# Entry of the down-projection: queue order of weights, operands, convolutions and loads

## The chip, the cores and the metric

The kernel runs on one core of one Trainium2 chip. The metric is the device time of one execution in microseconds; the time before is the median of three runs. The profile shows one execution: TensorE (PE) does the matmuls, ScalarE (ACT), VectorE (DVE) and GpSimd (POOL) the elementwise work, and SyncE (SP) issues most of the DMAs. Each engine works through its own queue in order, and so does SP: what waits at the head of a queue holds what is behind it.

## The reference

One decoder layer on a sequence of 1024 positions of width 1024, in float32: an RMSNorm, two attention mixers with gates and a residual addition, and then the part that matters here:

```
xn = rmsnorm(x, norm_ffn_w)
u = xn @ w_up                                  # 1024 -> 2 * 2816
c = conv_b + sum_j upad[:, j:j + S] * conv_w[j]  # causal, width 3, per channel
gate, val = split(c, 2)
x = x + (silu(gate) * val) @ w_down            # 2816 -> 1024
out = rmsnorm(x, norm_final_w)
```

## The kernel before

Activations lie transposed, channels on the 128 partitions and positions along the free dimension (T = 1024, in halves of H2 = 512). Every float32 matmul is done as three fp32r matmuls: each operand is split into a head (a cast, by ACT) and the rest (source less head, by DVE), and head x head, head x rest and rest x head are summed. For weights the two parts are `wh` and `wl` (`load_w`, lines 139 and 141), for operands of the down-projection the two halves of `h` (`split`, lines 820 and 821). Two by two blocks are multiplied in Strassen's manner with seven products, P1 to P7, whose operands are sums of blocks.

**Up-projection** (`hidden`). 22 iterations, j = 0 to 21, each a pair of weight columns and seven products of twelve matmuls (line 901). `recombine` (lines 460 to 467) sums the products into two tiles `us`. `glu` then does, for each of the pair, `conv`: a product with the norm's scale by POOL (line 1047), the first tap with the bias on ACT (line 1056), two further taps on DVE (lines 1058 and 1059); then silu on ACT (line 1039), a product on DVE (line 1040) and a store of the hidden row tile to `hd` in DRAM (line 1041). Three `glu` calls at the end are put off into the list `self.defer`: the second half of j = 20 and both halves of j = 21. The argument `after` makes such a call's POOL product wait for an instruction, the `wl` of some weight.

**Down-projection** (`down`). Its loop runs over steps i = 0, 1, 2, ...: for each of the products P1, P2, P5, P6, P3, P7, P4 two cuts of the 11 row tiles of a block (6 and 5), and for each cut four column blocks m. A step is 18 or 15 matmuls at line 1112: P1 is steps 0 to 7 (written as `y`), P2 is steps 8 to 15 (written as `d`). A step needs its weights and six or five operands. After a chain's second cut its bank is added to `x3`, the residual, by DVE (line 1118), one step later.

A step of the loop issues, in this order of the program: `next_w` (it keeps two steps of weights split: ACT's cast and DVE's rest of the following step, and the raw loads, at line 129, of two more); its matmuls; at steps 2, 10, 18 and 26 a load of 1 MB of the residual from `x2d` (line 1149); the loads of raw hidden tiles from the table `loads` (`fetch_h`, line 999: tiles `ha`, `hb`, `hc` for the blocks B11, B12 and B21/B22); as many operand preparations as the table `count` or a rule says (`prep`, calling `operand`: for P5 the subtraction at line 1020, for P6 the one at line 1022, and then the split); a deferred `glu` at the steps in `DEFER`; a late store of `hd` at the steps in `STORE`; evictions.

The six operands of P1's first cut are loaded during j = 20 (line 971) into tiles of the up-projection. The other five, B11 6 to 10, are loaded at steps 0 and 1. `open_down` makes the pools of the raw tiles (`hrp`, 11 buffers of each kind) in the space of the up-projection's operands, and one of the pools of split operands (`hp`, HP buffers); the other (`hpb`, HPB buffers) lies in the space of the up-projection's split weights and `us` tiles.

What sets the order. The program is a list; a planner with a cost model for each instruction lays out each engine's queue before the run, taking what it holds to be ready, the earliest in the list first. `tc.high_priority(n)` moves a block's instructions n places forward in that order. `with tc.issue_after(ins):` forces the block's instructions that are on the engine of `ins` to stand behind it in that engine's queue. Nothing is reordered during the run. `self.front`, a pair of instructions, does the same for the first ACT and the first DVE operation of the next convolution.

Of the kernel before, what the change touches and what calls it, by code (L numbers as in the profile page):

```python
# [22 lines left out]
H2 = 512  # L23
DFF = 2816
NF = DFF // P
EPS = 1e-6
RAW = 3
HP, HPB, HR = 6, 14, 11
STORE = (1, 6)
DEFER = (2, 5)  # L30
HK = NF // 2
# [13 lines left out]
class Trunk:  # L45
# [858 lines left out]
    def hidden(self, pair):  # L904
        nc, tc = self.nc, self.tc
        with ExitStack() as ctx:
# [11 lines left out]
            for j in range(NF):  # L918
                w, ps = ready.pop(j) if j else (w0, {})
                if j == 0:  # L920
# [4 lines left out]
                    for k in range(4):  # L925
                        hi, lo = self.split(*(xc2.tile([P, T], F32R, name=f"T42_{k}{p}") for p in "hl"), self.t42[k])
                        self.B["T4", k], self.B["T2", k] = ((hi[:, c], lo[:, c]) for c in (slice(0, H2), slice(H2, T)))
                    self.tctx.close()
                    tp = e(tc.tile_pool(name="tp", bufs=2, side="right", reuse_waits="tile"))
# [21 lines left out]
                if j == NF - 1:  # L951
                    self.defer.pop(0)(lo)
                    self.xctx2.close()
                    self.uw = None
                    self.open_down()
                    self.deep = True
                    with tc.high_priority(100):
                        self.ahead(2)
                self.recombine(ps, us, tp, 2)
                if j < NF - 1:  # L960
# [19 lines left out]
                if j > NF - 3:  # L980
                    self.front = None

                for w in range(2):
                    f = lambda after=None, j=j, w=w, us=us: self.glu(j, w, us[w], tp, after)
                    if j + w < NF - 1:
                        f()
                    else:
                        self.defer.append(f)

    def open_down(self):  # L990
        tc = self.tc
        self.dctx = ExitStack()
        self.hrp = self.dctx.enter_context(tc.tile_pool(name="hrp", bufs=HR, reuse_waits="tile"))
        self.hp = self.dctx.enter_context(tc.tile_pool(name="hp", bufs=HP, reuse_waits="tile"))
        self.nh = 0

# [46 lines left out]

    def conv(self, m, us, tp, after=None):
        nc = self.nc
        nc.gpsimd.memset(us[:, 0:2], 0.0)
        i = (nc.vector if m % NF == 0 else nc.gpsimd).tensor_tensor(us[:, 2:], us[:, 2:], self.rstd, ALU.mult)  # L1047
        if after is not None:
            self.tc.add_manual_dep(i.ins, after.ins.name, mybir.DependencyInfo(mybir.DependencyClass.Sync, mybir.DependencyReason.DATA), reason="later")
        c = self.tl(self.cpl, [P, T], "c")  # L1050
        cw = [self.vecs[:, C_CW + 3 * m + k:C_CW + 3 * m + k + 1] for k in range(3)]

        cast, low = [self.tc.issue_after(i) for i in self.front] if self.front else [nullcontext()] * 2
        self.front = None
        with cast:
            nc.scalar.activation(c, us[:, 2:], AF.Identity, bias=self.vecs[:, C_CB + m:C_CB + m + 1], scale=cw[2])  # L1056
        with low:
            nc.vector.scalar_tensor_tensor(c, us[:, 1:T + 1], cw[1], c, ALU.mult, ALU.add)  # L1058
        nc.vector.scalar_tensor_tensor(c, us[:, 0:T], cw[0], c, ALU.mult, ALU.add)  # L1059
        return c  # L1060

    def down(self):

        nc, tc = self.nc, self.tc
        with ExitStack() as ctx:
# [3 lines left out]
            self.hpb = e(tc.tile_pool(name="hpb", bufs=HPB, side="right", reuse_waits="tile"))  # L1069
            self.B, self.R = {("P1", k): self.hs[k] for k in range(6)}, {}  # L1070
            tt = nc.vector.tensor_tensor
# [7 lines left out]
            def fetch(name, *ks):  # L1079
                for k in ks:  # L1080
                    self.fetch_h(name, k)
# [34 lines left out]
            def evict(ps, m, hf, done):  # L1116
                x = col(m, hf)
                tt(x, x, ps, ALU.subtract if m > 3 else ALU.add)
                if done:
# [4 lines left out]

            loads = {0: [("B11", 6, 7, 8)], 1: [("B11", 9, 10)], 2: [("B21", 0, 1)], 3: [("B21", 2, 3)], 4: [("B21", 4, 5)], 5: [("B21", 6, 7)],
                     6: [("B21", 8, 9)], 7: [("B21", 10), ("B11", 0)]}
            for k in range(11):
                loads.setdefault(8 + k // 2, []).append(("B12", k))
                loads.setdefault(14 + k // 2, []).append(("B22", k))
            for k in range(1, 6):  # L1130
                loads[7 + k].insert(0, ("B11", k))
            count = {0: 3, 1: 2, 3: 1, 6: 3, 7: 2}
            chains, owed, tail, i = [{}, {}], [], [], 0
            for stage in STAGES:
                which, start, o, hf, done = plan[stage]
                for c in range(2):
                    for m in range(4):
                        if stage == "P4" and c == 1 and m > 1:
                            break
                        with tc.high_priority(150 if i < 4 else 0):  # L1140
                            w = self.next_w()
# [5 lines left out]
                        if i % 8 == 2 and i < 32:  # L1147
                            r, h = ((0, 0), (4, 1), (0, 1), (4, 0))[i // 8]
                            nc.sync.dma_start(x3[:, r:r + 4, h * H2:(h + 1) * H2], self.x2d[r:r + 4, :, h * H2:(h + 1) * H2].rearrange("m p t -> p m t"))
                        if i > 1:  # L1150
                            for l in loads.get(i, ()):
                                fetch(*l)
                        for k, _ in again:
                            fetch("B21", k)
                        again.clear()
                        if i < 2:
                            fetch(*loads[i][0])
                        prep(count.get(i, 0) if i < 8 else 2 if i % 4 < 2 or i < 16 else 1)
                        if i in DEFER:
                            self.defer.pop(0)(lo)  # L1160
                        if i in STORE:
# [136 lines left out]
```

## Time and profile before

| | us |
|---|---|
| median of three runs | 1335.62 (1335.47 to 1339.52) |
| profiled execution | 1335.52 |
| span of its profile | 1333.7 |
| PE busy | 1312.1 |
| DVE busy | 1056.9 |
| ACT busy | 621.2 |
| POOL busy | 479.5 |

The span runs from the first to the last instruction of the profile. Busy times of engines overlap each other. Matmuls are pipelined: an interval from start to start is the time that one costs, and the duration of a record, about 0.39 us, is longer than that. In a row of the timeline the first number is the start, the second the duration; a bracket at its end gives how long the engine had been idle just before and what it had waited for.

### The profile page before, as it was taken

The page shows a single profiled execution, that of the slowest core. Times are in us where ns is not written, and L with a number is a line of the kernel's source. Part 1 is how long each engine was busy: PE and PEld are TensorE (multiplying, and loading weights), DVE is VectorE, ACT ScalarE, POOL GpSimd, SP SyncE. Part 2 cuts the span into 40 slices and gives each one's busy share as a digit, 9 for nine tenths or more (in the row PEclk, how much of TensorE's full clock was granted, in tenths as well). Part 3 has the DMA queues.
Part 4 walks back from the last instruction along what each step waited for, and adds up shares of the span by engine and source line. Part 5 has one row for each costly group of instructions (what it writes and reads, how often), then busy time and mean ns, then how long its engine had stood idle before and what let it go on. Part 6 is the DMA issues. An engine that isn't in the chain of part 4 may idle for free.

```text
span 1333.7 us, 17123 instructions
## 1 busy us (share of the span) xinstructions
PE 1312.1 (98%) x6210; PEld 1090.0 (82%) x6210; DVE 1056.9 (79%) x1456; ACT 621.2 (47%) x967; POOL 479.5 (36%) x364
## 2 busy tenths in 40 slices
PE   9999999999999999999999999999999997999997
PEld 7888888888888878888888888888888885788886
DVE  8846775389898976455669999999999996998545
ACT  9432232276667774334444343334343434554543
POOL 0446652000101015641446666756666621000002
PEclk9999999999999999999999999999999999999998
DMA  7334342966553245234424336644635228864334
GB/s 259 129 147 153 141 158 111 274 173 190 143 149 136 76 143 223 101 122 142 151 90 180 121 138 166 145 186 123 220 101 150 71 91 274 303 204 155 96 97 146
DMA packets 71588, 205.96 MB, mean 154 GB/s; under 512 B 8016, under 2 KB 15824, under 8 KB 71376
## 3 DMA queue, kind: packets, MB, share of 16 engines
q1 hardware_dynamic: 57472, 176.03, 38.9%
q0 software_dynamic: 2304, 11.54, 4.5%
q10 hardware_dynamic: 11728, 17.31, 3.6%
q8 instruction: 49, 0.80, 0.2%
q14 instruction: 35, 0.29, 0.1%
HBM read 156.08 MB, written 71.83 MB: 171 GB/s over the span
## 4 chain that ended last, share of the span: by engine, by line
PE 82%; DVE 7%; issue 4%; DMA 2%; POOL 2%; ACT 2%; SPq 0%; POOLq 0%; DVEq 0%; ACTq 0%
PE t L901 32%; PE y L1112 7%; PE d L1112 7%; PE g L160 4%; PE g L161 4%; PE g L162 4%; PE sc L161 3%; PE sc L162 3%; PE sc L160 3%; PE sc L633 3%; DVE wl L120 1%; DVE c L1058 1%; PE t L649 1%; DVE c L1059 1%; PE t L752 1%
## 5 line engine op out<-in xcount | busy, mean ns | idle before, releaser
L141 DVE TENSOR_TENSOR wl<-raw,wh 128x1024 fp32r<-128x1024 f32 (+2 forms) x85 | 97.3, 1145 | 52.7 <-ACT wh L139 43.0
L139 ACT CAST wh<-raw 128x1024 fp32r<-128x1024 f32 (+2 forms) x85 | 74.1, 873 | 130.2 <-PE y L1112 53.5
L1047 POOL TENSOR_TENSOR us<-us,rstd 128x1024 f32<-128x1024 f32 x42 | 93.4, 2257 | 58.4 <-DVE us L466 31.5
L1056 ACT ACTIVATE c<-us,vecs 128x1024 f32<-128x1024 f32 x44 | 54.8, 1248 | 121.9 <-POOL us L1047 113.0
L120 DVE TENSOR_TENSOR sl<-sf,sh 128x1024 fp32r<-128x1024 f32 x62 | 95.9, 1548 | 14.7 <-ACT sh L118 14.7
L118 ACT CAST sh<-sf 128x1024 fp32r<-128x1024 f32 x62 | 64.7, 1046 | 85.7 <-PE t L901 44.0
L177 POOL TENSOR_TENSOR rs<-ms,mhalf 128x8 f32<-128x8 f32 (+2 forms) x9 | 13.3, 1474 | 235.8 <-DVE ms L175 229.7
L104 POOL TENSOR_TENSOR sf<-rv 128x512 f32<-128x512 f32 x30 | 54.9, 1830 | 117.6 <-DMA rv<-in_w_up 57.4
L1112 PE MATMUL y<-h,wh 128*128 128x512 f32 (+1 forms) x324 | 96.1, 380 | 0.0
L1112 PE MATMUL d<-h,wh 128*128 128x512 f32 x264 | 81.3, 389 | 0.2 <-ACT wh L139 0.2
L1059 DVE SCALAR_TENSOR_TENSOR c<-us,vecs,c 128x1024 f32<-128x1024 f32 x44 | 74.4, 1724 | 0.0
L160 PE MATMUL g<-xh,wh 128*128 128x512 f32 x176 | 70.9, 403 | 1.5 <-ACT g L562 1.5
L161 PE MATMUL g<-xl,wh 128*128 128x512 f32 x176 | 70.3, 400 | 0.0
L162 PE MATMUL g<-xh,wl 128*128 128x512 f32 x176 | 70.3, 399 | 0.0
L1112 PEld LDWEIGHTS y<-h,wh 128*128 128x128 f32 x324 | 60.1, 190 | 11.3
L106 POOL TENSOR_TENSOR sf<-raw,rv 128x512 f32<-128x512 f32 x30 | 54.9, 1830 | 35.6 <-DVE sl L120 35.6
L1058 DVE SCALAR_TENSOR_TENSOR c<-us,vecs,c 128x1024 f32<-128x1024 f32 x44 | 64.3, 1490 | 4.1 <-ACT c L1056 3.9
L1112 PE MATMUL y<-h,wl 128*128 128x512 f32 (+1 forms) x162 | 61.9, 382 | 3.3 <-DVE wl L141 3.2
L120 DVE TENSOR_TENSOR wl<-raw,wh 128x1024 fp32r<-128x1024 f32 (+1 forms) x32 | 62.8, 1962 | 0.1
L637 DVE CUSTOM_DVE_ANT_0 L<-sc,bias 128x128 f32<-128x128 f32 (+7 forms) x64 | 47.7, 750 | 17.0 <-PE sc L633 13.7
L616 POOL MEMSET aT<- 128x128 f32 x32 | 6.2, 206 | 151.7 <-PE t L662 97.9
L638 ACT ACTIVATE L<-L,sm 128x128 f32<-128x128 f32 (+7 forms) x64 | 49.6, 778 | 19.9 <-DVE sm L637 17.3
(394 smaller groups left out, 4159.3 us busy)
## 6 DMA issues: line engine op xcount, KB each, us to landing
u<-qd SPq DMA_DIRECT2D x72, 256.0 KB, 6.2
raw<-in_w_up SPq DMA_DIRECT2D x23, 512.0 KB, 4.9
raw<-in_w_in SPq DMA_DIRECT2D x22, 512.0 KB, 3.8
hd<-c SPq DMA_DIRECT2D x22, 512.0 KB, 2.6
sdP<-in_w_down POOLq DMA_DIRECT2D x16, 704.0 KB, 9.2
rv<-in_w_up SPq DMA_DIRECT2D x21, 512.0 KB, 4.6
hc<-hd SPq DMA_DIRECT2D x33, 256.0 KB, 5.3
gr<-gd SPq DMA_DIRECT2D x16, 512.0 KB, 3.4
```

The source lines that it names most:

```text
L118: cast = nc.scalar.copy(hi, src)
L120: low = nc.vector.tensor_tensor(lo, src, hi.bitcast(F32), ALU.subtract)
L139: self.hi = nc.scalar.copy(wh, raw)
L141: self.lo = (eng or nc.vector).tensor_tensor(wl, raw, wh.bitcast(F32), ALU.subtract)
L160: nc.tensor.matmul(ps, wh[:, kc + o, :], ah, start=first and n == 0, stop=False)
L161: nc.tensor.matmul(ps, wh[:, kc + o, :], al, start=False, stop=False)
L162: nc.tensor.matmul(ps, wl[:, kc + o, :], ah, start=False, stop=last and n == len(kcs) - 1)
L901: nc.tensor.matmul(ps, (ah, ah, al)[p][:, k, :], (bh, bl, bh)[p], start=first and n == p == 0, stop=last and p == 2 and n == len(ks) - 1, ...
L1047: i = (nc.vector if m % NF == 0 else nc.gpsimd).tensor_tensor(us[:, 2:], us[:, 2:], self.rstd, ALU.mult)
L1058: nc.vector.scalar_tensor_tensor(c, us[:, 1:T + 1], cw[1], c, ALU.mult, ALU.add)
L1059: nc.vector.scalar_tensor_tensor(c, us[:, 0:T], cw[0], c, ALU.mult, ALU.add)
L1112: nc.tensor.matmul(ps, v[:, k - k0, :], x, start=start and k == i == 0, stop=k == HK - 1 and i == 2, skip_group_check=True)
```

## The change

It changes the order around the entry of the down-projection, j = 21 and steps 0 to 7, and ties operand preparations to weights in all steps.

- At j = 21 the five loads B11 6 to 10 are issued ahead of the next weights, and the first deferred `glu` comes after these weights, with `self.front` set: its ACT and DVE taps stand behind the weights' cast and rest.
- The scale product of the last two convolutions is a function of its own, `scaled`, called at steps 2 and 4; the rest of each convolution follows one step later (3 and 5), with `self.front` set to that step's weights.
- The table `loads` starts with B21 0 to 5 at steps 0 and 1. The weights of step 1's `next_w`, where they are on SP, stand behind the last of the loads of step 0, and the residual's loads stand behind the last operand load.
- In every step the preparations stand behind the latest `wh` and `wl` on ACT and DVE.
- One operand preparation moves from step 6 to step 4. The pools of split operands have 7 and 13 buffers where they had 6 and 14.

```diff
-HP, HPB, HR = 6, 14, 11
+HP, HPB, HR = 7, 13, 11
 STORE = (1, 6)
-DEFER = (2, 5)
+DEFER = (2, 4)
...
                 if j == NF - 1:
-                    self.defer.pop(0)(lo)
                     self.xctx2.close()
                     self.uw = None
                     self.open_down()
                     self.deep = True
                     with tc.high_priority(100):
+                        for k in range(6, HK):
+                            self.fetch_h("B11", k)
                         self.ahead(2)
+                    self.front = self.hi.ins, self.lo.ins
+                    self.defer.pop(0)(lo)
                 self.recombine(ps, us, tp, 2)
...
-    def conv(self, m, us, tp, after=None):
+    def scaled(self, m, us, after=None):
         nc = self.nc
         nc.gpsimd.memset(us[:, 0:2], 0.0)
         i = (nc.vector if m % NF == 0 else nc.gpsimd).tensor_tensor(us[:, 2:], us[:, 2:], self.rstd, ALU.mult)
         if after is not None:
             self.tc.add_manual_dep(i.ins, after.ins.name, mybir.DependencyInfo(mybir.DependencyClass.Sync, mybir.DependencyReason.DATA), reason="later")
+
+    def conv(self, m, us, tp, after=None):
+        nc = self.nc
+        if m % NF < NF - 1:
+            self.scaled(m, us, after)
         c = self.tl(self.cpl, [P, T], "c")
...
-            loads = {0: [("B11", 6, 7, 8)], 1: [("B11", 9, 10)], 2: [("B21", 0, 1)], 3: [("B21", 2, 3)], 4: [("B21", 4, 5)], 5: [("B21", 6, 7)],
-                     6: [("B21", 8, 9)], 7: [("B21", 10), ("B11", 0)]}
+            loads = {0: [("B21", 0, 1, 2)], 1: [("B21", 3, 4, 5)], 4: [("B21", 6, 7)], 6: [("B21", 8, 9)], 7: [("B21", 10), ("B11", 0)]}
...
-            count = {0: 3, 1: 2, 3: 1, 6: 3, 7: 2}
+            count = {0: 3, 1: 2, 3: 1, 4: 1, 6: 2, 7: 2}
...
-                        with tc.high_priority(150 if i < 4 else 0):
+                        with tc.high_priority(150 if i < 4 else 0), tc.issue_after(self.load.ins) if i == 1 else nullcontext():
                             w = self.next_w()
                         lo = self.lo
...
                         if i % 8 == 2 and i < 32:
                             r, h = ((0, 0), (4, 1), (0, 1), (4, 0))[i // 8]
-                            nc.sync.dma_start(x3[:, r:r + 4, h * H2:(h + 1) * H2], self.x2d[r:r + 4, :, h * H2:(h + 1) * H2].rearrange("m p t -> p m t"))
-                        if i > 1:
-                            for l in loads.get(i, ()):
-                                fetch(*l)
+                            with tc.issue_after(self.load.ins):
+                                nc.sync.dma_start(x3[:, r:r + 4, h * H2:(h + 1) * H2], self.x2d[r:r + 4, :, h * H2:(h + 1) * H2].rearrange("m p t -> p m t"))
+                        for l in loads.get(i, ()):
+                            fetch(*l)
                         for k, _ in again:
                             fetch("B21", k)
                         again.clear()
-                        if i < 2:
-                            fetch(*loads[i][0])
-                        prep(count.get(i, 0) if i < 8 else 2 if i % 4 < 2 or i < 16 else 1)
+                        with tc.issue_after(self.hi.ins), tc.issue_after(lo.ins):
+                            prep(count.get(i, 0) if i < 8 else 2 if i % 4 < 2 or i < 16 else 1)
                         if i in DEFER:
+                            self.scaled(NF - 1, self.us[len(self.defer) % 2], lo)
+                        if i - 1 in DEFER:
+                            self.front = self.hi.ins, lo.ins
                             self.defer.pop(0)(lo)
```

5 lines of the change are left out of this document (3 added, 2 removed).

## The prediction

> **What bounds the kernel now.** I read the page's slices first, then TensorE's (PE's) busy time by stage, then the order of instructions on each engine in the one stage with holes.
>
> ```profile
> span 1333.7 us, 17123 instructions
> PE   9999999999999999999999999999999997999997
> DVE  8846775389898976455669999999999996998545
> ```
>
> PE is full in every slice but the last, which is the final normalisation and is not touched, and the 34th (some 1100 to 1133 us): the entry of the down-projection. VectorE (DVE) is nearly as full around it. A change there can win only what PE loses there. The next view counts the matmuls of line 1112 by stretch: time, PE busy (x count), weight loads busy (x count), granted clock, share of the DMA engines, GB/s.
>
> ```profile
> 1097.88:1101.96 4.08, 4.08 (x18) 3.19 (x17) 1.00 0.82 286
> 1101.96:1140.04 38.08, 29.27 (x115) 22.05 (x115) 0.96 0.85 281
> 1140.04:1175.00 34.96, 34.72 (x153) 28.45 (x152) 1.00 0.91 306
> ```
>
> The first row is step 0: 18 matmuls in 4.08 us, 0.2267 us each. Steps 1 to 3 have 18, steps 4 to 7 have 15 (five operands), 114 in all: 25.84 us at that pace. The second row took 38.08 us: **12.2 us lost**. The starts of the steps in PE's timeline (start, duration, in brackets the idle time before and what ended it) say where.
>
> ```profile
> 1095.16 0.39 PE L901 MATMUL t<-B_0h,sh 128*128 128x512 f32 x1
> 1103.41 0.73 PE L1112 MATMUL y<-sh,wh 128*128 128x512 f32 x2 [1.30 <-ACT wh L139]
> 1105.48 0.51 PE L1112 MATMUL y<-sh,wl 128*128 128x512 f32 x1 [1.34 <-DVE wl L141]
> 1112.02 0.73 PE L1112 MATMUL y<-sh,wh 128*128 128x512 f32 x2 [2.61 <-ACT wh L139]
> 1116.78 0.62 PE L1112 MATMUL y<-sh,wh 128*128 128x512 f32 x2
> 1120.86 0.61 PE L1112 MATMUL y<-h,wh 128*128 128x512 f32 x2
> 1125.07 0.62 PE L1112 MATMUL y<-h,wh 128*128 128x512 f32 x2
> 1128.87 0.62 PE L1112 MATMUL y<-h,wh 128*128 128x512 f32 x2
> 1132.27 0.61 PE L1112 MATMUL y<-h,wh 128*128 128x512 f32 x2
> 1135.62 0.80 PE L1112 MATMUL y<-h,wl 128*128 128x512 f32 x1 [2.74 <-DVE wl L141]
> 1138.66 0.62 PE L1112 MATMUL y<-h,wh 128*128 128x512 f32 x2
> 1140.90 0.73 PE L1112 MATMUL d<-h,wh 128*128 128x512 f32 x2 [0.24 <-ACT wh L139]
> ```
>
> Steps 1 and 2 together run 1101.96 to 1116.78, 14.8 us for 8.2: 6.6 lost, about half in each. Step 4 (1120.86 to 1125.07) loses 0.8, step 5 0.4, step 7 (1132.27 to 1140.04) 4.4, of which 1.45 is slow clock: seven matmuls from 1135.62 to 1138.66 in 3.04 us for 1.59. Step 8 adds 0.4 (1140.90 should be 1140.49). Sum 12.6 us. Every wait is for a weight part (wh, its fp32r head by ScalarE, ACT; wl, the rest, by DVE), never for raw data. What stood ahead of them in the queues:
>
> ```profile
> 1101.40 1.24 ACT L1056 ACTIVATE c<-us,vecs 128x1024 f32<-128x1024 f32 x1 [3.26 <-POOL us L1047]
> 1102.55 0.81 ACT L139 CAST wh<-raw 128x768 fp32r<-128x768 f32 x1
> 1109.14 0.62 ACT L820 CAST h<-ha 128x512 fp32r<-128x512 f32 x1 [5.78 <-DMA ha<-hd]
> 1111.14 0.83 ACT L139 CAST wh<-raw 128x768 fp32r<-128x768 f32 x1
> 1118.63 1.24 ACT L1056 ACTIVATE c<-us,vecs 128x1024 f32<-128x1024 f32 x1 [2.01 <-POOL us L1047]
> 1100.53 0.68 DVE L465 TENSOR_TENSOR u<-t,u 128x512 f32<-128x512 f32 x1
> 1102.67 1.29 DVE L1058 SCALAR_TENSOR_TENSOR c<-us,vecs,c 128x1024 f32<-128x1024 f32 x1 [1.47 <-ACT c L1056]
> 1104.47 0.95 DVE L141 TENSOR_TENSOR wl<-raw,wh 128x768 fp32r<-128x768 f32 x1
> 1131.65 1.39 DVE L1020 TENSOR_TENSOR ha<-ha,hb 128x512 f32<-128x512 f32 x2 [4.62 <-DMA hb<-hd]
> 1134.75 0.82 DVE L141 TENSOR_TENSOR wl<-raw,wh 128x640 fp32r<-128x640 f32 x1
> ```
>
> A convolution waiting for GpSimd (POOL) holds back step 1's weights; an operand cast waiting for its load holds back step 2's; the second convolution delays steps 4 and 5; an operand of a much later stage, waiting for its load, holds back step 7's.
>
> **The change part by part.** No arithmetic is added or removed; the same instructions change places.
>
> Step 1: the convolution's ACT and DVE parts now stand behind wh and wl of step 1. That wh needs its buffer, free when the P4 product of the last up-projection step ends (1095.16), so it can run before the POOL result of 1101.4. Its wl may stand behind the recombination's operations on DVE. At best the loss is 0; at worst L465 ends at 1101.1, two more of its kind (0.6 each) and the wl go first and end at 1103.2, when the third matmul wants it at 1102.4: 0.8. I take 0.4, of 3.2.
>
> Step 2: the five ha loads move ahead, and on SP past a weight load, the 1 MB residual load and another weight load that waited for wl.
>
> ```profile
> 1085.05 0.32 SPq L1041 DMA_DIRECT2D hd<-c  x1
> 1097.93 0.39 SPq L1149 DMA_DIRECT2D x<-x2d  x1
> 1105.45 0.34 SPq L129 DMA_DIRECT2D raw<-in_w_down  x1
> 1105.85 2.32 SPq L999 DMA_DIRECT2D ha<-hd  x5
> ha<-hd SPq DMA_DIRECT2D x11, 256.0 KB, 4.8
> x<-x2d SPq DMA_DIRECT2D x2, 1024.0 KB, 7.0
> ```
>
> They can leave after 1085.05 instead of 1105.85 and land near 1093, 4.8 us after issue; five issues hold SP 2.3 us, and the next weight load is not due until 1097.5. The ACT wait of 5.78 goes: 3.4 of PE.
>
> The residual load is the one that pays: it now stands behind six operand loads and a weight load that waits for step 1's wl, and perhaps behind a store that needs L1040. It leaves between 1103 and 1108 and lands 7 us later, by 1115. Its first reader is the eviction after step 4, which PE would now end at 1117.6. Hidden; if it were later still, DVE would block as it did for hb, 4.6 us.
>
> Steps 4 and 5: the POOL product is issued one step before the rest of its convolution, so 2 us of POOL lie beside a whole step of PE, and what follows stands behind the step's weights: 1.2 gone, at worst still there. POOL has nothing queued behind it; its product also waits for a wl, as before.
>
> Step 7: operand preparations now stand behind their step's newest wh and wl, so the 4.6 us wait for hb cannot stand ahead of them: 4.4, and step 8's 0.4, gone. The pool sizes (7 and 13) and counts move one preparation from step 6 to step 4: no cost beside the DVE sum below.
>
> What is late next is **DVE**.
>
> ```profile
> 1101.20:1140.20 39.00, 30.19 (x120) 22.62 (x119) 27.45 (x32) 16.90 (x24) 4.16 (x3) 0.96 0.85 284
> 1140.20:1200.00 59.80, 59.56 (x264) 48.97 (x263) 58.87 (x93) 36.51 (x59) 0.00 (x0) 1.00 0.73 245
> 1138.41 1.89 DVE L821 TENSOR_TENSOR h<-hc,h 128x512 fp32r<-128x512 f32 x3
> L141 DVE TENSOR_TENSOR wl<-raw,wh 128x640 fp32r<-128x640 f32 x8 | 6.5, 816 | 0.0
> ```
>
> The third busy figure is DVE's: 27.45 us in the stretch whose matmuls need 25.84. Less the two L1020 (1.4) and one wl (0.9), which leave it, and plus two preparations (1.3, at 1.89 for three) due sooner, it is 26.4. So DVE is full and in order: 0.6 too much by the count, with a few tenths for each wait on wh. I take 1.1 beside the 0.4 of step 1; ends 0 (the leftovers wait until after step 8) and 4 (a new wait as long as the old ones).
>
> From step 8 on, preparations may no longer run ahead of their step's weights. Before, DVE ran flat out to 1200 (second row) and PE lost nothing. Now steps 8 to 12 leave DVE idle, while 13 to 16 ask for two preparations of two operations (2.5), a wl (0.8), an eviction and a norm addition (0.6 each), 4.5 us in steps of 3.4, or of 4.1 for the last. Without the addition in the first, that is 0.5 + 1.1 + 1.1 + 0.4 = 3.1 us behind. A wl can be late by 3.4 + 0.45 - 0.7 (its wh) - 0.8 = 2.3 us before PE waits (2.7 in an 18-matmul step). I take 0.6; ends 0 and 3.
>
> Loads: steps 8 to 12 ask for 6.9 MB (five weight loads, ten of hb, five of ha, the second residual MB) in 19.7 us, 350 GB/s, and the stretches above moved 281 to 306 at a DMA share of 0.85 to 0.91. At 306 they take 22.5 us: 2.8 late, against a lead of one to two steps (3.4 to 8 us). I take 0.4; ends 0 and 2.8. [...]
>
> Sum: 12.6 - 0.4 - 1.1 - 0.6 - 0.4 = **10.1 us**. The profiled execution took 1335.52 us (span 1333.7 and 1.8 around it): 1325.4. The median of the runs, 1335.62, is 0.1 above it: **1325.5**.
>
> The waits left I charge at their length alone: the 2.61 us one was followed by matmuls at the full pace, only the 2.74 us one by a slow clock. [...]
>
> **The rivals.** *A wait stays or a new one takes its place*: the queues' order is planned, not measured, and one block of the old kind survives, as a cast behind a late operand or DVE behind the residual load. For it: four of five losses were such misplacements. Against: the new orders name just these pairs. One costs 3 to 4.5 us beyond my terms: 1328.5 to 1330.
>
> *The whole hole returns*: steps 1 to 7 are paced by a full DVE, which pays for each in-order wait, so PE loses about what it lost before: 10 to 13 us, 1333 to 1336, no change. Against: DVE idled 11.5 us of that stretch, and the waits it idled on are the ones moved.
>
> *Slower*: preparations that can no longer run ahead wait for their loads in DVE's queue. hb lands 5.5 us after issue in the median.
>
> ```profile
> hb<-hd SPq DMA_DIRECT2D x11, 256.0 KB, 5.5
> DMA to landing us min/median/max: 3.1/5.4/7.2
> ```
>
> If an operand is issued only one step (3.4 us) ahead and lands at the maximum, 7.2, DVE waits 3.8, 1.5 beyond the 2.3 that a wl can be late. Over the twelve steps 11 to 22 that is 18 us, 8 more than is won: 1343. It decides from 0.85 us a step. For it: the hb wait at 1131.65 shows such a block. Against: SP issued these loads two to three steps ahead, and nothing in the change holds operand loads back.
>
> **How the numbers follow.** My forecast (1322.9 to 1328) 0.62; one wait left (to 1331.5) 0.18; hole returns 0.08; slower 0.12. A measurement here tells about 0.3%, 4 us, from no change: faster (under 1331.6) 0.80; same 0.08; slower 0.12. The range is 1322.5 (all 12.6 won, and 0.4 for its uncertainty) to 1333, which takes in the first rival whole and the start of the second.
>
> **What would show it.** Right: ha issued before 1097; step 1 and 2's first matmuls without an idle time over 1 us; L1056 behind L139 on ACT; step 8 near 1128 to 1130; granted clock 1.00 throughout; DVE full from 1101 to 1130 without a DMA wait. Wrong: PE waiting for wl in steps 13 to 18 (the tied preparations), L1118 waiting for x<-x2d (the residual load), or DVE waiting for ha or hb (the loads). The prediction fails if the sum of PE's idle times after 1097 does not fall by some 8 us.

## The result, and the profile after

The changed kernel takes 1329.67 us in the median of seven runs (1328.35 to 1333.21), the kernel before 1337.49 in seven beside them (1334.09 to 1339.52). The ratio is 0.9947 with a 95% interval of 0.9931 to 0.9963: faster by 0.5%, some 7.1 us (the two medians lie 7.8 apart). The forecast was 1325.5 us, 10.1 us won, in a range of 1322.5 to 1333: faster, as said, but by less.

The profiled execution of after took 1328.35 us, the shortest of the seven; its span is 1326.6 us. The two spans divide at the first matmul of step 0 and the first of step 8:

| us | before | after | difference |
|---|---|---|---|
| start to step 0 | 1097.88 | 1099.81 | +1.93 |
| steps 0 to 7 | 42.16 | 33.75 | -8.41 |
| step 8 to the end | 193.66 | 193.04 | -0.62 |
| span | 1333.7 | 1326.6 | -7.1 |

At the full pace of 0.2267 us a matmul, the 132 matmuls of steps 0 to 7 need 29.92 us. The loss there was 12.24 us and is 3.83. First the page of after, busy tenths in 40 slices:

```profile
PE   9999999999999999999999999999999999999997
DVE  8846775289888976445669999999999998896865
PEclk9999999999999999999999999999999999999999
```

The hole in the 34th slice has gone from PE's row. The next view gives two stretches of after, steps 0 to 7 and the 41 us behind them: time, then busy us (x count) of PE, weight loads, DVE, ACT and POOL, granted clock, DMA share, GB/s.

```profile
1099.81:1133.56 33.75, 30.56 (x133) 24.62 (x132) 28.78 (x38) 17.10 (x26) 6.38 (x3) 1.00 0.85 299
1133.56:1175.00 41.44, 41.44 (x183) 34.07 (x182) 36.20 (x56) 25.23 (x39) 0.00 (x0) 1.00 0.95 325
```

PE misses 3.2 us in the first and nothing in the second. The granted clock is 1.00 in both. PE's timeline of after shows where the 3.2 us lie (rows as before: start, duration, idle time and what ended it):

```profile
1099.81 0.61 PE L1121 MATMUL y<-sh,wh 128*128 128x512 f32 x2
1103.89 0.63 PE L1121 MATMUL y<-sh,wh 128*128 128x512 f32 x2
1105.07 0.50 PE L1121 MATMUL y<-sh,wl 128*128 128x512 f32 x1 [0.55 <-DVE wl L141]
1108.85 0.61 PE L1121 MATMUL y<-sh,wh 128*128 128x512 f32 x2
1112.10 0.50 PE L1121 MATMUL y<-sh,wl 128*128 128x512 f32 x1 [2.64 <-DVE wl L141]
1115.88 0.62 PE L1121 MATMUL y<-sh,wh 128*128 128x512 f32 x2
1133.56 0.62 PE L1121 MATMUL d<-h,wh 128*128 128x512 f32 x2
```

Step 1 (1103.89 to 1108.85) takes 4.96 us for 4.08, so it loses 0.88. Step 2 (to 1115.88) takes 7.03 and loses 2.95. Steps 3 to 7, 78 matmuls, take 17.68 us, which is the full pace. So step 2 still waits as long as it did (2.61 before, 2.64 now), but for another engine: for DVE's rest instead of ACT's head. DVE's queue in after, and ACT's cast of step 2's weights, say why:

```profile
1098.89 0.95 DVE L141 TENSOR_TENSOR wl<-raw,wh 128x768 fp32r<-128x768 f32 x1
1099.76 0.68 DVE L462 TENSOR_TENSOR u<-t,s 128x512 f32<-128x512 f32 x1
...
1103.48 0.68 DVE L467 TENSOR_TENSOR us<-u,t 128x512 f32<-128x512 f32 x1
1104.07 0.95 DVE L141 TENSOR_TENSOR wl<-raw,wh 128x768 fp32r<-128x768 f32 x1
1105.03 1.29 DVE L1067 SCALAR_TENSOR_TENSOR c<-us,vecs,c 128x1024 f32<-128x1024 f32 x1
1106.23 0.69 DVE L466 TENSOR_TENSOR us<-t,u 128x512 f32<-128x512 f32 x1
1106.83 1.28 DVE L1068 SCALAR_TENSOR_TENSOR c<-us,vecs,c 128x1024 f32<-128x1024 f32 x1
1108.15 1.23 DVE L1044 TENSOR_TENSOR c<-c,c 128x1024 f32<-128x1024 f32 x1
1109.29 1.89 DVE L821 TENSOR_TENSOR h<-ha,h 128x512 fp32r<-128x512 f32 x3
1111.10 0.95 DVE L141 TENSOR_TENSOR wl<-raw,wh 128x768 fp32r<-128x768 f32 x1
1106.46 0.83 ACT L139 CAST wh<-raw 128x768 fp32r<-128x768 f32 x1
```

DVE stands still nowhere here: it waits for nothing from 1098.89 until step 2's wl is done. The head of step 2's weights was ready at 1107.29, but 2.95 us of other work, the product L1044 and three operand preparations that no step needs yet (1108.15 to 1111.10), stand ahead of step 2's wl. From SP's queue of after:

```profile
1099.86 0.33 SPq L129 DMA_DIRECT2D raw<-in_w_down  x1
1100.29 2.28 SPq L1003 DMA_DIRECT2D ha<-hd  x5
1105.05 7.36 SPq L129 DMA_DIRECT2D raw<-in_w_down  x2
1116.22 0.97 SPq L1158 DMA_DIRECT2D x<-x2d  x1
```

The five ha loads left at 1100.29, not soon after 1085: a load of weights stands ahead of them, and it left at 1099.86, when step 0's wl (1098.89, 0.95) was done. They left 5.6 us sooner than before all the same. The residual left at 1116.22: the second of the two weight loads that held SP from 1105.05 on left only when step 2's late wl was done, and operand loads, a store and one more weight load followed it.

### The profile page after: what moved, and what is told of

It reads as the page before. It is cut to its first block, busy times and chain, and to the rows that moved or that the text cites. A ratio compares the mean times of both kernels' runs of the same rounds, so it can differ in the third digit from the quotient of the medians.

```text
span 1326.6 us, 17120 instructions
## 1 busy us (share of the span) xinstructions
PE 1309.5 (99%) x6210; PEld 1088.9 (82%) x6210; DVE 1057.2 (80%) x1456; ACT 621.1 (47%) x967; POOL 480.4 (36%) x364
## 5 line engine op out<-in xcount | busy, mean ns | idle before, releaser
L1065 ACT ACTIVATE c<-us,vecs 128x1024 f32<-128x1024 f32 x44 | 54.8, 1247 | 115.5 <-POOL us L1051 109.9
L120 DVE TENSOR_TENSOR sl<-sf,sh 128x1024 fp32r<-128x1024 f32 x62 | 92.7, 1496 | 15.6 <-ACT sh L118 15.6
L104 POOL TENSOR_TENSOR sf<-rv 128x512 f32<-128x512 f32 x30 | 58.0, 1935 | 116.6 <-DVE sl L120 51.1
L120 DVE TENSOR_TENSOR wl<-raw,wh 128x1024 fp32r<-128x1024 f32 (+1 forms) x32 | 69.1, 2159 | 0.1
```

The lines of the kernel that those rows point to most:

```text
L104: tt(sa[:, 0], v[:, 0], v[:, 1], ALU.add)
L120: low = nc.vector.tensor_tensor(lo, src, hi.bitcast(F32), ALU.subtract)
```

## The experiments

In each, "the part from step 0" is the time from the first matmul of step 0 to the end of the span: 235.82 us before, 226.79 after. Where no median is given, the kernel was timed once, and the text goes by the parts of that one profile. Unless a kernel is said to be built otherwise, it is the changed kernel with the edit shown. Line numbers shift by a few from kernel to kernel.

**The first deferred convolution ahead of the weights, as it was.**

```diff
                 if j == NF - 1:
+                    self.defer.pop(0)(lo)
                     self.xctx2.close()
...
                         self.ahead(2)
-                    self.front = self.hi.ins, self.lo.ins
-                    self.defer.pop(0)(lo)
                 self.recombine(ps, us, tp, 2)
```

> The changed kernel with one part undone: the first deferred convolution is issued ahead of step 1's weights again, without the pair that puts its taps behind them. Down part, that is from step 0's first matmul to the end of the span: before 235.8 us, changed 226.8. Theory (each stall is one misplaced instruction in an in-order queue): ACT's tap waits for the GpSimd product ahead of step 1's cast, and step 1 loses 3.2 us as before instead of 0.9; step 2 loses less, 1 to 2 instead of 2.95, since vector work gets done in the stall; down part 228 to 229. Rival (a full vector engine paces steps 1 to 7, so the order within them does not matter): the two steps together lose 3.8 as in the changed kernel, down part 226.8.

The part from step 0 took 228.19 us. PE's timeline of this run has two waits, both in step 1:

```profile
1106.65 0.73 PE L1120 MATMUL y<-sh,wh 128*128 128x512 f32 x2 [1.69 <-ACT wh L139]
1108.71 0.50 PE L1120 MATMUL y<-sh,wl 128*128 128x512 f32 x1 [1.33 <-DVE wl L141]
```

Step 1 loses 3.6 us, step 2 nothing; then the clock is halved for some 3.4 us (0.50 granted from 1110.71 to 1112.71), which costs another 1.6. The part lies in the theory's range only by this clock: the 1 to 2 us that it expected at step 2 didn't come. Without the clock the two steps together lose about what they lose in the changed kernel (3.8), as the rival has it. The order of weights and convolution moves the wait from one step to the other and hardly shortens it: until step 2's wl, DVE has the same work to do.

**The residual's load where it stood in the program.**

```diff
-                            with tc.issue_after(self.load.ins):
+                            if True:
                                 nc.sync.dma_start(x3[:, r:r + 4, h * H2:(h + 1) * H2], self.x2d[r:r + 4, :, h * H2:(h + 1) * H2].rearrange("m p t -> p m t"))
```

> The changed kernel with the residual's loads free to stand ahead of the operand loads (the queue then has the first 1 MB directly ahead of the five ha loads, with no weight load between). Theory (loads were held by the queue's order, not by bandwidth): ha lands some 3 us later, about 1108, the cast of the first operand waits 2 to 3 us on ACT ahead of step 2's weights, step 2 loses 4 to 5.5 us instead of 2.95; the later wait of the vector engine for the residual (2.1 us) goes. Down part 228 to 229.5. Rival (the residual's place does not matter, only the weight loads that stood between did): down part 226.8, within 0.5.

The part from step 0 took 228.32 us. The residual left SP at 1101.74, just ahead of the ha loads, so that an operand's cast waited 1.60 for its load on ACT. Step 2 waited 0.52 for wh and 1.85 for wl: a loss of 2.9 for 2.95, divided otherwise, where the theory expected 4 to 5.5. Its wl came 11.26 us after step 0's start, in the changed kernel 11.29. So the place of the residual decides nothing while DVE is late there; the 1.5 us by which the part is longer are a halved clock behind step 2 (0.57 granted from 1113.28 to 1115.28, 0.58 to 1117.28), and this edit loses no more than the changed kernel with its clock halved (below). DVE's later wait for the residual is gone, as expected, and PE won nothing by it.

**The five ha loads issued at steps 0 and 1 again.**

```diff
                     with tc.high_priority(100):
-                        for k in range(6, HK):
-                            self.fetch_h("B11", k)
                         self.ahead(2)
...
-            loads = {0: [("B21", 0, 1, 2)], 1: [("B21", 3, 4, 5)], 4: [("B21", 6, 7)], 6: [("B21", 8, 9)], 7: [("B21", 10), ("B11", 0)]}
+            loads = {0: [("B11", 6, 7, 8), ("B21", 0, 1, 2)], 1: [("B11", 9, 10), ("B21", 3, 4, 5)], 4: [("B21", 6, 7)], 6: [("B21", 8, 9)], 7: [("B21", 10), ("B11", 0)]}
```

> The changed kernel with the five ha loads issued in steps 0 and 1 as before, instead of ahead of step 1's weights. In the queue the first three keep their place, and the last two stand behind a weight load. Theory (the five loads leave only when step 0's weights are split, so that issuing them earlier in the program buys little): step 2's loss stays within 0.7 of 2.95 us, down part 226.5 to 227.5. Rival (the early issue is what removed step 2's wait): step 2 loses 4 us or more, down part 228 or more.

The part from step 0 took 228.56 us, with the changed kernel's two waits (0.59 and 2.64) and a halved clock behind the second (0.50 granted from 1115.34 to 1117.34). Three of the loads now leave at 1101.84 and two at 1106.98. ACT waits 2.82 for one of them at 1112.09, behind the casts that step 2 needs, and PE pays nothing for it. DVE's queue of this run is the changed one, 1.5 us later like its step 0:

```profile
1109.69 1.23 DVE L1042 TENSOR_TENSOR c<-c,c 128x1024 f32<-128x1024 f32 x1
1110.83 1.89 DVE L821 TENSOR_TENSOR h<-ha,h 128x512 fp32r<-128x512 f32 x3
1112.64 0.95 DVE L141 TENSOR_TENSOR wl<-raw,wh 128x768 fp32r<-128x768 f32 x1
```

The part lies outside the theory's 226.5 to 227.5 and inside the rival's range, but step 2's wait is the changed kernel's to 0.01, and the clock is the difference. Loads that go out at steps 0 and 1, ahead of the residual, are soon enough; that they are issued during j = 21 buys nothing here.

**Preparations not tied to the weights.**

```diff
-                        with tc.issue_after(self.hi.ins), tc.issue_after(lo.ins):
+                        if True:
                             prep(count.get(i, 0) if i < 8 else 2 if i % 4 < 2 or i < 16 else 1)
```

> The changed kernel with operand preparations free again, not behind their step's weights. Theory (the tie only keeps preparations that wait for loads from standing ahead of weights): preparations run ahead of step 2's rest by one more, step 2 loses 3 to 4 us; from step 8 on the first subtraction for P5 may wait for its load, at most 1 us of PE. Down part 227 to 229. Rival A (the tie is what removed step 7's 4.4 us): step 7 loses 2 us or more again, down part 229 to 232. Rival B (the tie costs something later): down part under 226.3.

The part from step 0 took 229.89 us. Step 2's wait is 3.20 (2.64 with the tie), a halved clock follows it (0.50 granted from 1112.81 to 1114.81), and a wait of 0.46 for wl stands at 1159.04, in step 14. Of the 3.1 us more than in the profile of after, 0.6 is step 2's wait, 1.6 the clock, and 0.9 lies behind step 8. The part is in rival A's range, but not for its reason: step 7's wait of 2.74 for wl didn't come back. In the changed kernel it is gone without the tie too.

**The product L1044 and three preparations one step later.**

```diff
-        nc.vector.tensor_tensor(self.c0, self.c0, c, ALU.mult)
+        finish = lambda c0=self.c0: nc.vector.tensor_tensor(c0, c0, c, ALU.mult)
+        if j == NF - 2:
+            self.held = finish
+        else:
+            finish()
...
-            count = {0: 3, 1: 2, 3: 1, 4: 1, 6: 2, 7: 2}
+            count = {1: 3, 2: 2, 3: 1, 4: 1, 6: 2, 7: 2}
...
+                        if i == 1:
+                            with tc.issue_after(lo.ins):
+                                self.held()
```

> The changed kernel with 3.1 us of vector work moved behind step 2's wl: the product of the first deferred glu (L1044, 1.2 us) and the first three operand preparations (1.9 us), which come one step later (counts 3, 2 at steps 1, 2 instead of 0, 1). Theory (step 2's loss is the vector queue's order: its wl starts 11.3 us after step 0, behind unbroken vector work, and is wanted by 9.5): its wl ends near 9.1, step 2 loses 0 to 0.3 instead of 2.95, no slow clock after it, steps 3 and 4 lose nothing; down part 223.8 to 224.5 against 226.8, and 2.5 to 4.5 us less than the changed kernel timed beside it. Rival (vector engine full: the loss only moves): steps 3 to 5 lose 2 to 3 us, down part 226 to 228, timed within 1 us of the changed kernel.

1327.61 us in the median of five runs, 1337.16 for the kernel before beside them: ratio 0.9932 (0.9919 to 0.9946). The part from step 0 took 226.04 us, the loss in steps 0 to 7 fell to 2.37. Step 2's wait is gone, and the granted clock stays at 1.00. Of the 1.46 us less in steps 0 to 7, 0.7 came back behind them. A new wait stands at step 5; PE, DVE (step 2's wl first) and POOL in this run:

```profile
1105.04 0.50 PE L1125 MATMUL y<-sh,wl 128*128 128x512 f32 x1 [0.57 <-DVE wl L141]
1121.85 0.50 PE L1125 MATMUL y<-h,wl 128*128 128x512 f32 x1 [0.88 <-DVE wl L141]
```
```profile
1107.99 0.95 DVE L141 TENSOR_TENSOR wl<-raw,wh 128x768 fp32r<-128x768 f32 x1
1118.46 1.28 DVE L1071 SCALAR_TENSOR_TENSOR c<-us,vecs,c 128x1024 f32<-128x1024 f32 x1 [3.17 <-ACT c L1069]
1120.98 0.82 DVE L141 TENSOR_TENSOR wl<-raw,wh 128x640 fp32r<-128x640 f32 x1
```
```profile
1112.83 4.32 POOL L1055 TENSOR_TENSOR us<-us,rstd 128x1024 f32<-128x1024 f32 x1 [9.15 <-DVE wl L141]
```

The scale product takes 4.32 us here, 2.00 in the changed kernel (at 1114.20, when DVE was idle). So the tap behind it on ACT, the tap behind that on DVE, and step 5's wl behind that are late. Step 2's wl now starts 8.23 us after step 0 for 11.29, which shows that what stood ahead of it was the cause of its wait. The part misses the theory's 223.8 to 224.5 and lies at the lower end of the rival's 226 to 228, since 1.2 us of loss moved to step 5. The median is 3.64 us below that of the changed kernel timed beside it (next run), as the theory has it and not the rival.

**The changed kernel again.**

> The changed kernel once more, for a time beside the last one's and for what varies from run to run. Theory (queues up to step 0 are the same as before the change, so the 1.9 us by which step 0 began later in its first profile is chance, and so is the slow clock after the step 2 wait, which that profile did not have): step 0 begins between 1097 and 1102, the waits of steps 1 and 2 are again 0.9 and 2.8 within 0.2, and the down part is 226.8, or 228.4 if matmuls after the wait run at half pace. Rival (the change itself delays what is ahead of step 0): step 0 begins at 1099.5 to 1101.5 here and never near 1098.

1331.25 us in the median of five runs beside the same runs of before; ratio 0.9958 (0.9945 to 0.9970). In its profile step 0 starts at 1100.75, which fits the theory and the rival alike, and the two waits are 0.56 and 2.60, as in the profile of after, but the part from step 0 takes 228.65 us. The view by stretch has the reason (time, PE busy, granted clock, DMA share, GB/s):

```profile
1113.00:1115.00 2.00, 1.98 (x6) 0.73 0.40 94
1115.00:1117.00 2.00, 2.00 (x6) 0.50 1.02 369
1117.00:1119.00 2.00, 2.00 (x9) 0.92 0.96 361
```

Behind the same wait the granted clock fell to half for some 3.4 us and cost about 1.6. In the profile of after it didn't.

**The last two convolutions in one piece again, at steps 2 and 5.**

```diff
-DEFER = (2, 4)
+DEFER = (2, 5)
...
-        if m % NF < NF - 1:
-            self.scaled(m, us, after)
+        self.scaled(m, us, after)
...
-                            self.scaled(NF - 1, self.us[len(self.defer) % 2], lo)
-                        if i - 1 in DEFER:
-                            self.front = self.hi.ins, lo.ins
                             self.defer.pop(0)(lo)
```

> The changed kernel with the last two convolutions whole again, at steps 2 and 5, their taps not behind the weights. Theory (misplaced taps wait for the GpSimd product ahead of weights): in the vector queue the first tap stands ahead of step 4's and of step 7's rest; step 4 loses 0.5 to 1 and step 7 1 to 3 us; down part 228 to 232 with a slow clock or two. Rival (those convolutions cost nothing once loads and preparations are in order): down part 226.8, or 228.4 with a slow clock after step 2's wait.

The part from step 0 took 229.61 us, 2.8 more than in the profile of after, with a granted clock of 1.00 in both. Steps 1 and 2 lose the same. Step 7 loses 1.3 (a wait of 0.70 for wl) and step 8 1.1. Step 4, where the kernel before lost 0.8 and the theory expected 0.5 to 1, loses nothing.

**The tie alone, put into the kernel before.**

```diff
-                        prep(count.get(i, 0) if i < 8 else 2 if i % 4 < 2 or i < 16 else 1)
+                        with tc.issue_after(self.hi.ins), tc.issue_after(lo.ins):
+                          prep(count.get(i, 0) if i < 8 else 2 if i % 4 < 2 or i < 16 else 1)
```

> The kernel before with one part of the change added: operand preparations behind their step's weights. Theory (the subtraction that waited for hb stood ahead of step 7's wl): that wait goes; the last convolution's tap still stands ahead of step 7's wl, which loses 1 to 2.5 us instead of 4.4; steps 1 and 2 lose their 6.6 as before. Down part 232 to 234.5 against 235.8. Rival (the tie does nothing alone): 235 to 236.5.

The part from step 0 took 233.58 us, 2.2 less than before. Step 7's wait is gone; PE's timeline has these left, and smaller ones of 0.3 and 0.9 at steps 2 and 8:

```profile
1106.80 0.73 PE L1112 MATMUL y<-sh,wh 128*128 128x512 f32 x2 [1.73 <-ACT wh L139]
1108.86 0.79 PE L1112 MATMUL y<-sh,wl 128*128 128x512 f32 x1 [1.33 <-DVE wl L141]
1115.89 0.73 PE L1112 MATMUL y<-sh,wh 128*128 128x512 f32 x2 [0.43 <-ACT wh L139]
1126.03 0.50 PE L1112 MATMUL y<-h,wl 128*128 128x512 f32 x1 [0.70 <-DVE wl L141]
```

A halved clock at step 1's waits lasts 6.8 us here, from 1107.8 to 1114.6 (0.50 granted from 1108.82 to 1112.82), and costs 2.7 more. The 1 to 2.5 us that the theory left at step 7 for the tap didn't come. So the tie alone removes step 7's wait, and it is one of two ways: without the tie, the other edits of the change together do so too.

**Step 5's weights ahead of the taps**, built on the kernel with both moved one step later: the rest of the last two convolutions comes at steps 4 and 5.

```diff
-                            self.scaled(NF - 1, self.us[len(self.defer) % 2], lo)
-                        if i - 1 in DEFER:
+                            self.scaled(NF - 1, self.us[DEFER.index(i)], lo)
+                        if i in (4, 5):
                             self.front = self.hi.ins, lo.ins
                             self.defer.pop(0)(lo)
```

> As the run with both edits (product L1044 and three preparations one step later), with the taps of the last two convolutions at steps 4 and 5 where they were at 3 and 5, so that step 5's wl stands ahead of the first tap, whose GpSimd product took 4.32 us. Theory (a wl waits only for what stands ahead of it in DVE's queue): the wait of 0.88 at step 5 goes, step 1's of 0.57 stays; the part from step 0 to the end takes 225.0 us for 226.04, loss in steps 0 to 7 about 1.3. Rival (DVE is full there, and work put behind one wl is ahead of the next): the wait comes back at step 6 or 7 with 0.5 to 1 us, and that part takes 225.8 to 226.3. Median against the kernel before: ratio about 0.9925 by the theory, 0.993 by the rival.

1327.00 us in the median of five, before 1337.08: ratio 0.9923 (0.9911 to 0.9936). The part from step 0 took 225.09 us. Step 5's wait is gone. A part of the rival came too: step 6 waits 0.27 for wl and loses 0.57, and step 7 loses 0.35. The interval overlaps that of the run before this edit, so the 0.6 us between the two medians isn't shown as a gain. DVE and POOL in this run:

```profile
1118.80 2.70 DVE L1071 SCALAR_TENSOR_TENSOR c<-us,vecs,c 128x1024 f32<-128x1024 f32 x1 [0.24 <-ACT c L1069]
```
```profile
1112.25 4.32 POOL L1055 TENSOR_TENSOR us<-us,rstd 128x1024 f32<-128x1024 f32 x1 [9.15 <-DVE wl L141]
1118.03 2.38 POOL L1055 TENSOR_TENSOR us<-us,rstd 128x1024 f32<-128x1024 f32 x1 [1.46 <-DVE wl L141]
```

The tap took 2.70 us for 1.28: it began while the second scale product ran.

**And one operation of the last recombination behind step 1's weights**, built on the run above.

```diff
-        tt(c21, u3, ps["P4"], ALU.subtract)
+        with self.tc.issue_after(self.lo.ins) if self.deep else nullcontext():
+            tt(c21, u3, ps["P4"], ALU.subtract)
```

> As the run before it, and L467 of the last recombination (0.6 us, DVE) behind the wl of step 1. Theory: step 1's loss of 0.85 falls to about 0.25 (its wl starts 0.6 us sooner), nothing else moves: the part from step 0 to the end takes 224.4 us. Rival: L467 frees the bank of the last product later, or PE's other wait at that place (0.1 to 0.3 us at the first matmuls of the down-projection) takes over: 225.0, no gain over the run before it.

1325.65 us in the median of five: ratio 0.9920 (0.9906 to 0.9933). The part from step 0 took 224.05 us, a little less than the theory's 224.4, and the loss in steps 0 to 7 is 1.08. Step 1 has no wait left; the only one in these steps is step 6's:

```profile
1122.15 0.50 PE L1126 MATMUL y<-h,wl 128*128 128x512 f32 x1 [0.27 <-DVE wl L141]
```

This kernel is below both that were compared, 1325.65 against 1329.67 and 1337. Its interval lies apart from the changed kernel's second one (from 0.9945) and just overlaps the first (from 0.9931); it isn't shown to be better than the run above, whose interval it shares.

**The kernel before again.**

> The unchanged kernel, for a second profile. Theory (the order of the queues fixes the waits; where step 0 starts and whether a slow clock follows a wait vary from one execution to another): step 0 starts between 1097 and 1103, the same three waits stand at steps 1, 2 and 7 (1.3 + 1.3, 2.6, 2.7 us within 0.5), and the part from step 0 to the end takes 235.8 us within 2. Rival (the profile of before was an unusual execution, and the change won less than its profile says): that part takes under 233 us.

Step 0 starts at 1098.66 and the part from it takes 235.44 us, within 0.4 of the first profile. The long waits stand at the same places, and three of them have other lengths (step 1's second is 1.33 for 1.34):

```profile
1104.61 0.73 PE L1112 MATMUL y<-sh,wh 128*128 128x512 f32 x2 [1.71 <-ACT wh L139]
1113.48 0.73 PE L1112 MATMUL y<-sh,wh 128*128 128x512 f32 x2 [2.88 <-ACT wh L139]
1136.49 0.50 PE L1112 MATMUL y<-h,wl 128*128 128x512 f32 x1 [1.74 <-DVE wl L141]
```

Step 7's is 1.74 where it was 2.74, half a us outside what was expected of it. Step 4's 0.51 is gone, and 0.91 stands at step 8. Here the granted clock is 0.51 from 1114.66 to 1116.66, behind step 2's wait, and 1.00 behind step 7's; in the first profile it was the other way round (1.00 from 1112.02 to 1116.02, 0.52 from 1135 to 1137).

## Why the prediction was right or wrong

The direction and the range were right: the waits named were removed, and the time lies 4.2 us above the forecast inside the range. Of these 4.2, 2.9 stand in the profiled execution, and the rest is the distance from it to the median. Step by step:

- **Step 1 (0.4 taken, 0.8 at worst): the worst case came.** It loses 0.88, by the path that was given as the upper end: L465, L467 and the wl in a row on DVE. The run with L467 behind that wl removed this.
- **Step 2 (3.4 won by the ha loads): the step that failed.** The 5.78 us wait of ACT went, as said, and PE won some 0.5 of the 3.4: DVE was nearly as late. The prediction had named DVE as what is late next, but its term of 1.1 us came from a sum over 39 us, in which DVE's work nearly fits. The excess lies in the first 13 us: the end of the recombination, a convolution, L1044 and three preparations, all ahead of the wl that PE wants at 1109.3. It measured 2.95, within the ends of 0 and 4. That these 2.95 us of work were the cause was shown by moving them, both parts together; that the order of loads was not, by issuing the loads late.
- **Where the loads would leave: wrong, without a price.** The ha loads left at 1100.29 instead of soon after 1085.05, and the residual at 1116.22 instead of 1103 to 1108. The prediction read the time at which SP had been free, not the load of weights that stands ahead of the block. DVE did wait for the residual, 2.08 us at 1124.31, against 4.6 named for that case; it is covered by the lead of the weights.
- **Steps 4 and 5 (1.2 won): right in place.** They run at the full pace. But the whole treatment of the convolutions is worth 2.8 us (two single profiles with a granted clock of 1.00), and without it the loss stands at steps 7 and 8, not at 4 and 5: the wait moves to where DVE's lead runs out.
- **Steps 7 and 8 (4.8 won): right.** Either the tie (alone in the kernel before) or the other edits (the changed kernel without it) remove step 7's wait, so the gains of the parts don't add.
- **From step 8 on (0.6 for tied preparations, 0.4 for loads): nothing was lost.** PE has no wait there up to 1300. The loads came: one 10 us stretch of after moved 395 GB/s, more than the 306 that the term was worked out from.

```profile
1140.00:1150.00 10.00, 10.00 (x46) 8.29 (x45) 6.82 (x11) 4.03 (x7) 0.00 (x0) 1.00 1.04 395
```

- **The clock (waits charged at their length alone): too cheap.** In the profile of after this holds. In the second profile of the same kernel, and in six of the seven other runs in which step 1 or 2 kept waits of over 1.3 us (all but the one with the convolutions in one piece), the clock was halved behind them, at about 1.6 us, and 2.7 with the tie alone. Over the seven timed executions of the changed kernel the mean granted clock goes the same way: the two at 0.998 took 1328.35 and 1328.82 us, the two at 0.996 took 1330.89 and 1333.21. One such stretch in the sum, at the 1.45 us that the prediction read behind step 7's wait, would have made 1327, which is nearer.
- **The start of step 0: not in the sum.** It came 1.93 us later in after. The queues of all five engines are the same in all the kernels here up to the last recombination. Between two profiles of one kernel it moved by 0.78 (before) and 0.94 (changed), over all of them from 1097.88 to 1102.69. With it goes a wait of PE in the up-projection, in the view of waits of after (in all, times, longest us):

```profile
PE t L901 <- DVE u L462: 1.3, 2, 0.7
```

  This wait is under 0.1 us in the first profile of before, 0.6 and 0.9 where step 0 starts at 1097.95 and 1098.66, 1.3 in both profiles of the changed kernel, and 1.8 at the latest start, 1102.69, but 1.9 and 1.8 also at 1100.71 and 1100.82. It explains a part of the shift; what makes it differ between executions of the same queues was not found. The start at 1100.82 is of the kernel before with the tie alone, so a late start doesn't need the change; that the change adds nothing to it isn't shown.

- **The signs.** Of those for right, three came: the convolution's tap (L1056, in after L1065) stood behind the cast on ACT, the first matmuls of steps 1 and 2 didn't wait, and the granted clock stayed at 1.00, in one profile of two. The others didn't: the ha loads left at 1100.29, not before 1097, and step 8 began at 1133.56, not at 1128 to 1130. Step 2's wait was not at its first matmul but at its third. Of the signs for wrong, DVE's wait for the residual came. PE's idle times after 1097, step 8's included, fell from 9.0 us to 3.2, by 5.8, where the prediction asked for some 8; the loss, which counts the halved clock and the slower matmuls behind a wait too (step 1 of after lost 0.88 with a wait of 0.55, step 2 2.95 with 2.64), fell by 8.4 in steps 0 to 7.
- **The rivals and the chances.** The time lies in the band of the first rival, a wait left or a new one in its place (1328.5 to 1330, chance 0.18), and not in the forecast's own (1322.9 to 1328, chance 0.62). Its mechanism came too: a new wait on DVE at step 2, as long as the old one. That the number falls in its band is partly luck: the new wait cost 1.85 beyond the term for DVE, not 3 to 4.5, and the later start of step 0 and the median's distance from the profile made up the rest.

The account of the profiles: 10.1 forecast; 0.5 more at step 1 and 1.85 more at step 2, 1.0 less from step 8 on, and 0.3 for small differences leave 9.03 for the part from step 0 (8.41 in steps 0 to 7, 0.62 behind); less the start of step 0, 1.93, this is the 7.1 of the spans. The second rival, that the whole hole returns, paced by a full DVE, was right about the mechanism at steps 1 and 2 and wrong about the rest: with 2.95 us of work out of the way of one wl the loss in steps 0 to 7 fell from 3.83 to 2.37, and with two more moves to 1.08.

## What to carry to other kernels

When a wait is removed, don't sum the next engine's work over the whole stretch: write its queue down to each deadline, and ask what of it stands ahead of the next thing that PE needs. Here DVE's work nearly fitted on the average, and yet PE lost 2.95 us to one late wl at step 2; what helped was to move the work that nobody needed yet behind that deadline, not to make loads sooner. Profile one kernel twice before a us or two is put down to an edit: between two profiles of one kernel the start of a stage moved by 0.78 and 0.94 us here, and the clock behind a wait cost about 1.6 or nothing.

## What the runs showed of the hardware

**The scale product on GpSimd and some of DVE's work took longer beside each other.** The product of 128x1024 took 2.00 us in after while DVE was idle (at 1114.20) and while it did the sums of the recombination (at 1101.72, beside L463 to L465 at 0.68 or 0.69 each, the length that L462 had before it). It took 4.32 beside DVE's weight rests and preparations, in the run with both moved one step later and in the one built on it. In the first of these runs DVE's row of work ends at 1115.28 and the product at 1117.15, 1.87 later: most of the 2.00 that it takes beside an idle DVE. The other way round, DVE's tap of 1.28 took 2.70 when it began 0.77 after a product had: the product ended at 1120.41, the tap 1.09 later. In the profile of before a preparation of 0.69 that began 0.05 after a product, at 1116.65, took 2.49. No run here changed DVE's work beside a product alone, so what makes the two slow each other was not shown.

**Behind waits of one length the granted clock was halved in some runs and 1.00 in others.** Behind 2.60 us it was halved (the changed kernel again), and behind 2.64 in the run with the late loads; behind 2.64 in after and in the run with the convolutions in one piece it was 1.00. Behind 1.69 and 1.33 with four tenths of work between them it was halved, behind 1.71 and 1.33 in the second profile of before it was 1.00. Where it was halved, the lowest stretch of 2 us read 0.50 to 0.57, and the stretches together lack as much as 3.4 us at 0.50 do; that cost 1.45 to 1.7 us of matmuls. With the tie alone it was twice as long, 6.8 us, and cost 2.7. In the second profile of before:

```profile
1114.66:1116.66 2.00, 2.00 (x6) 1.50 (x6) 1.90 (x3) 1.89 (x4) 0.00 (x0) 0.51 0.86 288
1116.66:1118.66 2.00, 2.00 (x7) 1.61 (x6) 1.81 (x3) 0.76 (x2) 0.80 (x1) 0.64 0.93 302
```

What decides it was not found: in two profiles of the changed kernel the same wait, 2.64 and 2.60, had a clock of 1.00 once and of 0.50 once. In steps 0 to 8 the profiles have 14 places with a wait of 1.3 to 3.2 us (step 1's two waits counted as one). At six the granted clock stayed at 1.00, at seven another 1.45 to 1.7 us was lost, and 2.7 at the one with the tie alone; so such a wait is to be charged at its length at least.
